# Up projection of a conv-GLU block: seven block products for eight over six of its sixteen contraction tiles, and low weight parts made by adding transfers

## Chip, cores and metric

One core of a Trainium2 chip runs the kernel. The metric is the time of one execution on the device in microseconds (us); the value shown is the median of three runs. Smaller is better.

## The reference

The layer has a token-mixing half and a gated MLP with a convolution. The change touches the MLP, over 512 latent tokens (8 rows of 64), model width 2048 and inner width 5632:

```python
z = h @ w_up                                   # (512, 2048) @ (2048, 11264)
grid = z.reshape(1, rows, GRID_W, 2 * D_FF)
grid = depthwise_3x3(grid, w_conv)             # per channel, SAME padding
val, gate = jnp.split(grid.reshape(1, n, 2 * D_FF), 2, axis=-1)
f_lat = (val * jax.nn.silu(gate)) @ w_down     # (512, 5632) @ (5632, 2048)
```

Ahead of it stand the modulation vectors from the conditioning, the input projection, pooling heads, a diagonal state-space scan and an output projection. After it stand a norm, a gate and the residual. The modulation vector that gates the MLP's output is needed only at the very end; its products run in the background of the MLP.

## The kernel before

**Split numbers.** Each large product is made of two-part operands: `hi` is the value rounded to TensorE's float32r form, `lo` the rest. `mm3` (L175) issues three matmuls for each pair of tiles: hi by hi, hi by lo, lo by hi. An activation tile `h2[k]` (16 of them, one for each contraction tile of 128) holds [hi, lo] of 128 rows by 512 tokens. A matmul has a stationary 128x128 weight tile and, in the MLP, 512 moving columns; only the first two passes of the MLP, whose token halves become ready one after the other (`up_half`), use 256 columns.

**Weight pages.** `Stream` hands weights out in pages of 128x1024 in one fixed order. `load` issues the DMA of a raw page on SP's queue. `make` rounds it on ScalarE into `whi` (L77), and VectorE subtracts to give `wlo` (L78). Rings of two buffers each hold `raw`, `whi` and `wlo`. `get` returns a page and first makes the one behind it (`ahead` 1), so a page is made while its predecessor is multiplied, in the buffers that the page two before it leaves.

**The MLP.** Channels go in 44 passes of 128 value and 128 gate channels. Pass i, `up(i)`, takes four pages (two for the value channels j=0, two for the gate channels j=1), 96 matmuls in all, into one PSUM bank for each j; ScalarE copies each bank into a padded image `zp` (L1345). `conv(i)` runs nine taps for each j on VectorE (L1309, L1311), then silu, product and split into `g`. Every fourth pass completes a group for the down projection: `down(gi, d)` takes two pages and 48 matmuls into four banks, and `evict` adds these to `facc` (L1359). From pass 5 on, one `down` stands behind nearly every `up`.

**Order.** Each engine runs its instructions in program order. TensorE's are written by `up` and `down`; the rest are generators (`Threads`) that get steps at `bg.tick(us)`, `share` (0.65 in the MLP) of the time given, by priority. PSUM has eight banks that rotate. `gemv5` streams the last modulation weights through four `gv` buffers (SP's queue, VectorE dots at L975), and `rows_of` spreads the result to `frow`.

Of the kernel before, what the change touches and what calls it, by code (L numbers as in the profile page):

```python
# [21 lines left out]
F32 = mybir.dt.float32  # L22
# [18 lines left out]
NGRP = NP // GRP  # L41


class Stream:


    def __init__(self, nc, pool, pages, ahead, dahead, bufs):
        self.nc, self.pool, self.pages, self.ahead, self.dahead = nc, pool, pages, ahead, dahead
        self.bufs = bufs
        self.raws, self.made, self.i = [], [], 0  # L50

    def load(self, upto):
        while len(self.raws) < min(upto, len(self.pages)):
            key, ap = self.pages[len(self.raws)]
            n = ap.shape[-1]
# [6 lines left out]

    def make(self, upto):
        nc = self.nc
        while len(self.made) < min(upto, len(self.pages)):
# [3 lines left out]
            n = ap.shape[-1]  # L69
            raw = self.raws[i]  # L70
            self.raws[i] = None
            if key[0] in ("df", "wo2"):
# [57 lines left out]
def emit(tc, A, out, xs_dram, dbg=None):  # L130
# [38 lines left out]

    def gvload(ap):  # L170
        r = ring.tile([128, 512], F32, name="gv", tag="gv", bufs=4)
        nc.sync.dma_start(r[:], ap)
        return r

    def mm3(o, ahi, alo, bhi, blo, start, stop):  # L175
        PE.matmul(o, ahi, bhi, start=start, stop=False)  # L176
        PE.matmul(o, ahi, blo, start=False, stop=False)  # L177
        PE.matmul(o, alo, bhi, start=False, stop=stop)  # L178

# [25 lines left out]
    for x in sched:  # L205
        if x[0] == "U" and x[1] >= NH:
            pages += [(("up", x[1], j), A["w_up"][x[1], j]) for j in range(4)]
# [3 lines left out]
    W = Stream(nc, ring, pages, 1, 1, (2, 2, 2))  # L211
    W.big = lambda name, dt=F32R: sb.tile([128, 1024], dt, name=name, tag="pg", bufs=NPG)
# [4 lines left out]
    pa = phA.enter_context(tc.tile_pool(name="pa", bufs=1))  # L217
    ph0 = ExitStack()
# [748 lines left out]
    def gv_dots(todo, row):  # L967

        tiles = []
        for x in range(len(todo)):  # L970
            while len(tiles) < min(x + 4, len(todo)):
# [105 lines left out]
    def rows_of(c, r, pool, tag, bufs):  # L1077
        dgs = pool.tile([128, 1024], F32, name="dg", tag=tag, bufs=bufs)
        for q in range(4):
            o = bank("rowb")  # L1080
            for k in range(4):
                dg = dgs[:, ((4 * q + k) % 8) * 128:((4 * q + k) % 8 + 1) * 128]
                V.tensor_scalar(dg, ident[:], acol[:, c, 4 * q + k:4 * q + k + 1], None, op0=OP.mult)
            yield 1.0, 0.3
            for k in range(4):
                dg = dgs[:, ((4 * q + k) % 8) * 128:((4 * q + k) % 8 + 1) * 128]
# [195 lines left out]

    frow = [pg(f"frow{j}", (2, 512)) for j in range(2)]

    def gemv5():
        for hf in range(2):
            sr = p2.tile([128, 1024], F32, name="srow2", tag="srow2", bufs=1)
            nc.sync.dma_start(sr[:], A["c_row"][:, hf * 1024:(hf + 1) * 1024])
            S.activation(sr[:], sr[:], AF.Silu)
            todo = [(3, nt, 2 * hf + q) for nt in range(16) for q in range(2)]  # L1290
# [256 lines left out]
```

## Time and profile before

| what | value |
|---|---|
| median of three runs | 2179.85 us (2173.26 to 2180.87) |
| the profiled execution | 2177.72 us |
| its span, first to last instruction | 2175.9 us |
| mean granted TensorE clock | 0.983 |
| busy share: PE, DVE, ACT, POOL | 97%, 69%, 32%, 11% |
| HBM read | 302.46 MB |

PE is TensorE's matmuls and PEld its weight loads, DVE is VectorE, ACT ScalarE, POOL GpSimd, SP the engine that issues most loads. A busy time counts an instruction from its start to its end; matmuls overlap, so the distance between two starts, not the duration of one, says what a matmul costs in a stream. The profiled execution lies 2.1 us under the median of the three runs.

### The profile page before, as it was taken

How to read it: one execution, taken by the hardware profiler on the slowest of the kernel's cores; microseconds unless marked ns; L12 is line 12 of the kernel's file. 1: busy time of each engine (PE TensorE's matmuls, PEld its weight loads, DVE VectorE, ACT ScalarE, POOL GpSimd, SP SyncE). 2: the span in 40 equal slices, each digit the busy share in tenths (PEclk: the TensorE clock that was granted, in tenths of full speed). 3: DMA queues.
4: the chain of work that ended last, by engine and by line, in shares of the span. 5: the costliest groups of instructions: out<-in, count | busy, mean ns of one | idle time of the engine just before them, and what ended most of it. 6: DMA issues, size and time to landing. Idle time of an engine off the chain costs nothing.

```text
span 2175.9 us, 25243 instructions
## 1 busy us (share of the span) xinstructions
PE 2102.5 (97%) x9708; PEld 1645.7 (76%) x9708; DVE 1493.3 (69%) x2183; ACT 694.4 (32%) x976; POOL 243.8 (11%) x311
## 2 busy tenths in 40 slices
PE   7998999999898999999999999999999999999996
PEld 3575777767777888888888888888888888888885
DVE  1573488436677788778778777676776767767676
ACT  3343424544356323322222222222222222222224
POOL 5951100142025000000000000000000000000004
PEclk8999999999999999999999999999999999999998
DMA  9876454657665223443343333232332233232225
GB/s 371 311 285 218 136 178 145 205 150 206 223 211 204 78 88 127 144 140 119 109 154 124 124 126 112 88 97 88 97 97 92 93 97 93 92 97 97 92 93 193
DMA packets 107672, 315.05 MB, mean 145 GB/s; under 512 B 15520, under 2 KB 21536, under 8 KB 103328
## 3 DMA queue, kind: packets, MB, share of 16 engines
q1 hardware_dynamic: 99776, 303.39, 42.0%
q10 hardware_dynamic: 7776, 10.06, 1.4%
q8 instruction: 76, 1.25, 0.2%
q14 instruction: 44, 0.36, 0.0%
HBM read 302.46 MB, written 10.94 MB: 144 GB/s over the span
## 4 chain that ended last, share of the span: by engine, by line
PE 65%; DVE 2%; ACT 1%; issue 1%; DMA 1%; DVEq 0%; POOL 0%; ACTq 0%
PE up L176 14%; PE up L178 14%; PE up L177 14%; PE dn L177 7%; PE dn L178 7%; PE dn L176 7%; ACT scr L1124 1%; DMA raw<-in_w_up 0%; PE uh L178 0%; DMA raw<-in_w_down 0%; DVE facc L1126 0%; PE uh L177 0%; PE uh L176 0%; DVE wlo L78 0%; DVE hf L1195 0%
## 5 line engine op out<-in xcount | busy, mean ns | idle before, releaser
L78 DVE TENSOR_TENSOR wlo<-raw,whi 128x1024 fp32r<-128x1024 f32 (+1 forms) x326 | 403.6, 1239 | 456.7 <-ACT whi L77 453.9
L77 ACT ACTIVATE whi<-raw 128x1024 fp32r<-128x1024 f32 (+1 forms) x326 | 341.5, 1048 | 787.2 <-PE dn L178 308.6
L1311 DVE SCALAR_TENSOR_TENSOR cv<-zp,wconv,cv 128x512 f32<-128x512 f32 x704 | 528.4, 751 | 18.8
L176 PE MATMUL up<-h,whi 128*128 128x512 f32 x1344 | 531.4, 395 | 0.0
L178 PE MATMUL up<-h,wlo 128*128 128x512 f32 x1344 | 530.9, 395 | 0.0
L177 PE MATMUL up<-h,whi 128*128 128x512 f32 x1344 | 530.8, 395 | 0.0
L178 PEld LDWEIGHTS up<-h,wlo 128*128 128x128 f32 x1344 | 251.9, 187 | 61.8
L176 PEld LDWEIGHTS up<-h,whi 128*128 128x128 f32 x1344 | 252.0, 187 | 61.4
L177 PEld LDWEIGHTS up<-h,whi 128*128 128x128 f32 x1344 | 251.9, 187 | 61.4
L177 PE MATMUL dn<-wlo,g 128*128 128x512 f32 x672 | 265.5, 395 | 0.0
L178 PE MATMUL dn<-whi,g 128*128 128x512 f32 x672 | 265.4, 395 | 0.0
L176 PE MATMUL dn<-whi,g 128*128 128x512 f32 x672 | 265.4, 395 | 0.0
L1126 POOL TENSOR_TENSOR facc<-facc,frow 128x512 f32<-128x512 f32 x11 | 15.4, 1422 | 1435.1 <-ACT scr L1124 1435.1
L1345 ACT ACTIVATE zp<-up 128x512 f32<-128x512 f32 x84 | 50.5, 601 | 378.5 <-PE up L178 378.5
L177 PEld LDWEIGHTS dn<-wlo,g 128*128 128x128 f32 x672 | 126.0, 187 | 30.8
L176 PEld LDWEIGHTS dn<-whi,g 128*128 128x128 f32 x672 | 125.9, 187 | 30.9
L178 PEld LDWEIGHTS dn<-whi,g 128*128 128x128 f32 x672 | 126.0, 187 | 30.7
L975 DVE SCALAR_TENSOR_TENSOR scr<-gv,srow 128x512 bf16<-128x512 f32 x132 | 97.4, 738 | 17.8 <-DMA gv<-in_ada_n 11.1
L1359 DVE TENSOR_TENSOR facc<-facc,dn 128x512 f32<-128x512 f32 x144 | 92.1, 680 | 0.7 <-PE dn L178 0.7
L176 PE MATMUL ub<-hT,whi 128*128 128x512 f32 x192 | 79.4, 414 | 1.9 <-ACT mt L585 1.9
L176 PE MATMUL wo<-whi,mx 128*128 128x512 f32 x192 | 79.5, 414 | 0.0
L177 PE MATMUL wo<-wlo,mx 128*128 128x512 f32 x192 | 77.4, 403 | 0.9 <-DVE wlo L78 0.9
(285 smaller groups left out, 2434.4 us busy)
## 6 DMA issues: line engine op xcount, KB each, us to landing
raw<-in_w_up SPq DMA_DIRECT2D x176, 512.0 KB
raw<-in_w_down SPq DMA_DIRECT2D x88, 512.0 KB
gv<-in_ada_n SPq DMA_DIRECT2D x132, 256.0 KB
adak<-in_ada_k SPq DMA_DIRECT2D x32, 1024.0 KB
gv<-in_ada_m SPq DMA_DIRECT2D x96, 256.0 KB
raw<-in_w_out SPq DMA_DIRECT2D x32, 512.0 KB
raw<-in_w_inp SPq DMA_DIRECT2D x24, 512.0 KB
adag<-in_ada_n SPq DMA_DIRECT2D x7, 1024.0 KB
```

Source lines behind the costliest of these rows:

```text
L77: nc.scalar.activation(hi[:, :n], raw[:, :n], AF.Copy)
L78: nc.vector.tensor_tensor(lo[:, :n], raw[:, :n], hi[:, :n].bitcast(F32), op=OP.subtract)
L176: PE.matmul(o, ahi, bhi, start=start, stop=False)
L177: PE.matmul(o, ahi, blo, start=False, stop=False)
L178: PE.matmul(o, alo, bhi, start=False, stop=stop)
L975: V.scalar_tensor_tensor(scr[:, :512], tiles[x][:], 1.0, row(qf), op0=OP.mult, op1=OP.mult, accum_out=gacc[:, qf, c, nt:nt + 1])
L1124: S.activation(scr[:, :512], m, AF.Square, accum_out=st8[:, t, d:d + 1])
L1126: eng.tensor_tensor(m, m, row[d // 2][:, d % 2, :], op=OP.mult)
L1311: V.scalar_tensor_tensor(a[:], zz, wcol, a[:], op0=OP.mult, op1=OP.add)
L1345: S.activation(zp[j][i % 2][:, 1:9, 1:65], o.rearrange("p (r c) -> p r c", r=8), AF.Copy)
L1359: V.tensor_tensor(f, f, os[t], op=OP.add)
```

## The change

**Seven products.** From pass 4 on (`NS`), `up7(i)` replaces `up(i)`. Ten of the 16 contraction tiles are multiplied as before (`plain`, four pages of 640 columns, 15 matmuls each). The other six are taken as three pairs; over value and gate channels, the two tiles of a pair and the two token halves of 256 this is a product of 2x2 blocks, done in Winograd's form with seven block products instead of eight (`half`, seven calls of nine matmuls with 256 columns). The sums of activation blocks are made once on POOL (`hsums`), those of weight blocks for each pass on VectorE, in place in the raw tiles (`make` after `sb`). The seven products go to four banks, and `csums` combines these into `zp`: one ScalarE copy and six VectorE adds in place of two ScalarE copies.

A pass now takes eight pages: up0 (640 columns), sa (768), up2, sb (384 of its 768 made), up1, up3, sA and sB (768 each, the summed blocks). The raw blocks of the pairs come in two tiles of their own (`load_pair`), loaded behind the making of the former pass's sB.

**Low parts.** For up, dn, sa and sb pages VectorE no longer subtracts: ScalarE writes the negated rounded page into `wlo`, and a transfer issued by POOL adds the page from DRAM onto it. For sA and sB (and the pages before the MLP) VectorE still subtracts.

**Order of matmuls.** `page_mm`, and `down` likewise, first issues all hi-by-hi and hi-by-lo matmuls of a page (two thirds), then all that read `wlo`.

**Room.** `gv` goes from four buffers to two, the second `cv` tile from two to one, `rows_of` and `gemv5` work in smaller pieces, and `frow` is made after the last pass.

The core of the diff (the fitting of buffers, layouts of the weights and the moved `frow` are left out):

```diff
 class Stream:
...
-            nc.scalar.activation(hi[:, :n], raw[:, :n], AF.Copy)
-            nc.vector.tensor_tensor(lo[:, :n], raw[:, :n], hi[:, :n].bitcast(F32), op=OP.subtract)
+            nc.scalar.activation(hi[:, c0:n], raw[:, c0:n], AF.Copy)
+            if key[0] in ("up", "dn", "sa", "sb"):
...
+                nc.scalar.activation(lo[:, c0:n], raw[:, c0:n], AF.Copy, scale=-1.0)
+                nc.gpsimd.dma_start(lo[:, c0:n], ap[:, c0:n], accum_op=OP.add)
+            else:
+                nc.vector.tensor_tensor(lo[:, c0:n], raw[:, c0:n], hi[:, c0:n].bitcast(F32), op=OP.subtract)
             self.made.append((key, hi, lo))
+            if key[0] == "sb":
...
+                nc.vector.tensor_tensor(a22, a21, a22, op=OP.add)
+                nc.vector.tensor_tensor(a21, a11, a21, op=OP.subtract)
+                nc.vector.tensor_tensor(a11, a22, a11, op=OP.subtract)
+                nc.vector.tensor_tensor(a12, a12, a11, op=OP.subtract)
+            nxt = self.pairs.get(key)
+            if nxt is not None:
+                self.load_pair(*nxt)
...
+    def page_mm(todo, start, stop):
...
+        for x, (o, ah, al, bh, bl) in enumerate(todo):
+            PE.matmul(o, ah, bh, start=start and x == 0, stop=False)
+            PE.matmul(o, ah, bl, start=False, stop=False)
+        for x, (o, ah, al, bh, bl) in enumerate(todo):
+            PE.matmul(o, al, bh, start=False, stop=stop and x == n - 1)
...
+    def hsums(late):
...
+        for p in range(SW):
+            k1, k2 = h2o[p], h2o[SW + p]
...
+            def full(o, h, c):
+                PO.tensor_tensor(o, h[:, 0, c].bitcast(F32), h[:, 1, c].bitcast(F32), op=OP.add)
+
+            def split(d, x):
+                PO.tensor_copy(d[:, 0], x)
+                PO.tensor_tensor(d[:, 1], x, d[:, 0].bitcast(F32), op=OP.subtract)
+            full(w[0], k1, H0)
+            full(w[1], k1, H1)
+            if late:
+                PO.tensor_tensor(w[0], w[1], w[0], op=OP.subtract)
+                split(k1[:, :, H1], w[0])
+                continue
+            full(w[2], k2, H1)
+            yield 0.0, 0.3
...
+    def csums(i, bk):
...
+        S.activation(z0[:, ha], v(p16[:, H0]), AF.Copy)
+        V.tensor_tensor(z1[:, ha], z0[:, ha], v(p16[:, H1]), op=OP.add)
+        V.tensor_tensor(z0[:, hb], z1[:, ha], v(p57[:, H0]), op=OP.add)
+        yield 0.7, 0
+        V.tensor_tensor(z1[:, ha], z1[:, ha], v(p57[:, H1]), op=OP.add)
+        V.tensor_tensor(z1[:, hb], z1[:, ha], v(p57[:, H0]), op=OP.add)
+        yield 0.7, 0
+        V.tensor_tensor(z0, z0, v(p23), op=OP.add)
+        yield 0.7, 0.3
+        V.tensor_tensor(z1, z1, v(yy), op=OP.add)
...
+    def up7(i):
...
+        plain(p23, 0, 0)
+        w = W.get(("sa", i))
+        half(p16[:, H0], w, 0, lambda p: h2o[p][:, :, H0], True, False)
+        half(p23[:, H0], w, 1, lambda p: h2o[SW + p][:, :, H0], False, False)
+        bg.tick(1.5)
+        plain(yy, 1, 0)
+        w = W.get(("sb", i))
+        half(yy[:, H0], w, 1, lambda p: tt["p", p][2], False, False)
+        bg.tick(0.7)
+        plain(p23, 0, 1)
+        plain(yy, 1, 1)
+        w = W.get(("sA", i))
+        half(p16[:, H1], w, 0, lambda p: tt["p", p][1], False, True)
+        half(p23[:, H1], w, 1, lambda p: h2o[SW + p][:, :, H1], False, True)
+        bg.tick(1.5)
+        w = W.get(("sB", i))
+        half(p57[:, H0], w, 1, lambda p: h2o[p][:, :, H1], True, False)
+        half(p57[:, H1], w, 0, lambda p: tt["p", p][0], False, True)
+        bg.tick(1.0)
+        cth[i] = bg.add(csums(i, bk), 1)
...
     for x in sched:
...
+            if x[1] == NH:
+                hs_t = bg.add(hsums(False), 0)
+            if x[1] == NS - 1:
+                bg.finish(hs_t)
+                W.load_pair(NS, [A["w_ups"][0, m] for m in range(2)])
+            if x[1] == NS:
+                bg.finish(bg.add(hsums(True), 0))
+                g5_t = bg.add(gemv5(), 3)
```

## Rows read from the trace of the kernel before

**Rows 1.** The profile's page: busy time, share of the span, instructions of each engine.

```profile
PE 2102.5 (97%) x9708; PEld 1645.7 (76%) x9708; DVE 1493.3 (69%) x2183; ACT 694.4 (32%) x976; POOL 243.8 (11%) x311
```

**Rows 2.** Busy time by stretch (us, instructions), granted clock, DMA share, GB/s.

```profile
core 0: us, PE busy (x) PEld busy (x) DVE busy (x) ACT busy (x) POOL busy (x), PEclk, DMA share, GB/s
640.00:724.00 84.00, 73.64 (x507) 67.45 (x506) 57.47 (x90) 52.41 (x91) 36.23 (x40) 0.94 0.49 181
724.00:2122.00 1398.00, 1398.00 (x6009) 1123.80 (x6009) 1036.57 (x1423) 365.75 (x445) 0.00 (x0) 1.00 0.33 107
2122.00:2176.00 54.00, 35.69 (x155) 28.70 (x153) 36.26 (x55) 22.56 (x46) 24.44 (x15) 0.86 0.53 195
1500.00:1800.00 300.00, 300.00 (x1287) 241.02 (x1286) 209.13 (x269) 74.62 (x90) 0.00 (x0) 1.00 0.30 95
```

**Rows 3.** PE in order of time: 512-column matmuls, twelve starts apart.

```profile
1830.34 0.40 PE L176 MATMUL dn<-whi,g 128*128 128x512 f32 x1
...
1832.91 0.39 PE L178 MATMUL dn<-whi,g 128*128 128x512 f32 x1
1833.14 0.40 PE L176 MATMUL up<-h,whi 128*128 128x512 f32 x1
```

**Rows 4.** All engines in order of time: 256-column matmuls, nine starts apart.

```profile
702.24 0.28 PE L176 MATMUL uh<-h,whi 128*128 128x256 f32 x1
...
703.29 0.28 PE L176 MATMUL uh<-h,whi 128*128 128x256 f32 x1
```

**Rows 5.** ScalarE, then VectorE, then SP in order of time: making a page, next load.

```profile
1833.34 1.06 ACT L77 ACTIVATE whi<-raw 128x1024 fp32r<-128x1024 f32 x1 [4.54 <-PE dn L178]
1834.43 1.23 DVE L78 TENSOR_TENSOR wlo<-raw,whi 128x1024 fp32r<-128x1024 f32 x1 [0.73 <-ACT whi L77]
1824.97 0.33 SPq L60 DMA_DIRECT2D raw<-in_w_up  x1
```

**Rows 6.** Busy time by stretch around that load, the only one under way.

```profile
1824.90:1825.90 1.00, 1.00 (x6) 0.78 (x5) 0.96 (x3) 0.00 (x0) 0.00 (x0) 1.00 0.00 0
1825.90:1826.40 0.50, 0.50 (x4) 0.40 (x3) 0.50 (x1) 0.00 (x0) 0.00 (x0) 1.00 1.15 180
...
1827.40:1827.90 0.50, 0.50 (x4) 0.41 (x3) 0.50 (x1) 0.16 (x1) 0.00 (x0) 1.00 0.67 270
1827.90:1828.40 0.50, 0.50 (x4) 0.41 (x3) 0.47 (x2) 0.50 (x1) 0.00 (x0) 1.00 0.00 0
```

**Rows 7.** Groups of instructions: ScalarE's copies by form.

```profile
L77 ACT ACTIVATE whi<-raw 128x1024 fp32r<-128x1024 f32 x318 | 336.0, 1057 | 776.1 <-PE dn L178 308.6 <-PE up L177 180.8 <-issue 133.9
L77 ACT ACTIVATE whi<-raw 128x768 fp32r<-128x768 f32 x4 | 3.4, 846 | 9.1 <-PE pp L177 5.3 <-PE ub L177 3.8
L1323 ACT ACTIVATE g<-cv 128x512 fp32r<-128x512 f32 x44 | 27.1, 617 | 5.5 <-DVE cv L1318 5.5
```

**Rows 8.** Groups of instructions: POOL's 256- and 512-column operations.

```profile
L1197 POOL TENSOR_TENSOR h<-hf,h 128x256 fp32r<-128x256 f32 x30 | 25.9, 899 | 15.6 <-ACT h L1193 15.5
L1126 POOL TENSOR_TENSOR facc<-facc,frow 128x512 f32<-128x512 f32 x11 | 15.4, 1422 | 1435.1 <-ACT scr L1124 1435.1
```

**Rows 9.** Groups of instructions of VectorE, 724 to 2122 us.

```profile
L78 DVE TENSOR_TENSOR wlo<-raw,whi 128x1024 fp32r<-128x1024 f32 x249 | 305.1, 1225 | 313.0 <-ACT whi L77 310.3
L1359 DVE TENSOR_TENSOR facc<-facc,dn 128x512 f32<-128x512 f32 x144 | 92.1, 680 | 0.7 <-PE dn L178 0.7
L1309 DVE TENSOR_SCALAR cv<-zp,wconv 128x512 f32<-128x512 f32 x88 | 42.3, 481 | 0.0
```

**Rows 10.** The page's DMA queues: packets, MB, share of 16 engines.

```profile
q1 hardware_dynamic: 99776, 303.39, 42.0%
q10 hardware_dynamic: 7776, 10.06, 1.4%
q8 instruction: 76, 1.25, 0.2%
q14 instruction: 44, 0.36, 0.0%
```

**Rows 11.** The chain that ended last, end of the kernel: start, us, what.

```profile
2127.66 3.45 DMA raw<-in_w_down
2131.13 1.07 ACT wbh L77
```

More of the change, by code (lines that the diff above doesn't have):

```diff
@@ L41 @@
 NGRP = NP // GRP
+SW = 3
+PW = (16 - 2 * SW) * 64
+NS = 4
+ORD = [*range(SW), *range(8, 8 + SW), *range(SW, 8), *range(8 + SW, 16)]
 class Stream:
@@ L970, in gv_dots @@
         for x in range(len(todo)):
-            while len(tiles) < min(x + 4, len(todo)):
+            while len(tiles) < min(x + gvp[1], len(todo)):
                 c, nt, qf = todo[len(tiles)]
@@ L1300, in conv @@
         for j in range(2):
+            while i > 1 - j and not cth[i - 2 + j][2]:
+                bg._step(cth[i - 2 + j])
             z = zp[j][i % 2]
-            a = p2.tile([128, 8, 64], F32, name=f"cv{j}", tag=f"cv{j}", bufs=2)
+            a = p2.tile([128, 8, 64], F32, name=f"cv{j}", tag=f"cv{j}", bufs=2 - j)
             ct = 44 * j + i
@@ L1327, in conv, with v @@
         yield 0.6, 0
-    cth, zfree = {}, set()
+    h2o = [h2[k] for k in ORD]
+    ev_t = []
+    cth, zfree, summed = {}, set(), set()
+    def csums(i, bk):
+        p16, p23, p57, yy = bk
+        bk.clear()
+        z0, z1 = [zp[j][i % 2][:, 1:9, 1:65] for j in range(2)]
+        ha, hb = slice(0, 4), slice(4, 8)
+        def v(a):
+            return a.rearrange("p (r c) -> p r c", c=64)
+        yield 0.0, 0.4
+        for j in range(2):
+            while (i - 2, j) not in zfree:
+                bg._step(cth[i - 2])
+        S.activation(z0[:, ha], v(p16[:, H0]), AF.Copy)
[8 more added lines that the diff above has]
+        V.tensor_tensor(z1, z1, v(yy), op=OP.add)
+        summed.add(i)
+        del p16, p23, p57, yy
+        yield 0.7, 0
+        yield from conv(i)
@@ new lines, in up7, with half, plain @@
+    def up7(i):
+        if i - 1 >= NS:
+            while i - 1 not in summed:
+                bg._step(cth[i - 1])
+        bk = [bank(f"u7{n}") for n in range(4)]
+        p16, p23, p57, yy = bk
+        def half(o, key, m, hs, start, stop):
+            whi, wlo = key
+            cs = [slice((m * SW + p) * 128, (m * SW + p + 1) * 128) for p in range(SW)]
+            page_mm([(o, whi[:, c], wlo[:, c], hs(p)[:, 0], hs(p)[:, 1]) for p, c in enumerate(cs)], start, stop)
+        def plain(o, j, n):
+            whi, wlo = W.get(("up", i, 2 * j + n))
+            nk = PW // 128
+            hs = [h2o[2 * SW + n * nk + k] for k in range(nk)]
+            page_mm([(o, whi[:, k * 128:(k + 1) * 128], wlo[:, k * 128:(k + 1) * 128], h[:, 0, :], h[:, 1, :])
+                     for k, h in enumerate(hs)], n == 0, j == 1 and n == 1)
+            bg.tick(3.3)
+        plain(p23, 0, 0)
[18 more added lines that the diff above has]
+        cth[i] = bg.add(csums(i, bk), 1)
+        if i == NP - 1:
+            h2[:] = [None] * KT
+            h2o.clear()
+            tt.clear()
+            frow.extend(pg(f"frow{j}", (2, 512)) for j in range(2))
+            fr2.append(bg.add(frows(), 0))
@@ L1331, in up, with frows @@
+    fr2 = []
+    def frows():
+        bg.finish(g5_t)
+        while NP - 1 not in summed:
+            bg._step(cth[NP - 1])
+        yield from rows_of(3, frow, p2, "srow2", 1)
     def up(i):
@@ L1367, in down @@
         if gi == NGRP - 1:
-            bg.finish(g5_t)
+            bg.finish(*fr2)
+        bg.finish(*(ev_t if fr2 else ev_t[:-1]))
         os = [bank(f"dn{t}") for t in range(4)]
```

124 lines of the change are left out of this document (93 added, 31 removed).

## The prediction

> **What bounds the kernel now.** I read the busy times on the page of the profile first, then the same split by stage, then instructions in order of time. The page of the profile gives PE 97% of the span, VectorE 69%, ScalarE 32% and POOL 11% [rows 1]. The stretches show where that is exact: from 724 to 2122 us, the MLP, PE is busy for 1398.00 of 1398.00 us at a granted clock of 1.00, while VectorE works 74%, ScalarE 26% and POOL not at all [rows 2]. So in this stage nothing but PE's own stream sets the time, and time won or lost in that stream counts in full. The duration of a matmul record (0.40 us) is not its price: twelve 512-column matmuls start within 2.80 us (1830.34 to 1833.14), 0.2333 us each [rows 3]. The change stands or falls with the price of 256 columns, and the first two passes show it: nine such matmuls, each with its own weight load, start within 1.05 us, 0.1167 us each, exactly half [rows 4].
>
> **The saving.** The six contraction tiles cost a pass 6 x 2 x 3 = 36 matmuls of 512 columns, 8.40 us; they now cost 7 x 9 = 63 of 256, 7.35 us. That is 1.05 us a pass, 42.0 us over the 40 passes from 4 to 43. The ten plain tiles keep their 60 matmuls (14.0 us). Reordering a page's matmuls changes their number nowhere.
>
> **What it asks of VectorE, ScalarE and memory.** For a pass and its `down`, VectorE loses six subtractions of 1.225 us (7.35 us) [rows 9]. It gains two of 768 columns (0.92 each by size), four weight sums of 384 (0.5 each by size), four half-image adds (0.4 each, about half of 0.68) and two whole ones (0.68): 6.8 us. So VectorE stays near 74%. ScalarE gains for low parts four copies of 640 columns, one of 768, one of 384 and two of 1024 (0.73, 0.85, 0.50, 1.06 us, by size between [rows 7]): 6.4 us in about 32.5, from 26% to some 45%. Late in the MLP the DMA engines move 95 GB/s at a share of 0.30 [rows 2]; the adding transfers bring about 3 MB more for each pass and its `down`, so the bandwidth stays. Each of these hides behind PE; what decides is whether a page's parts arrive in time.
>
> **When a low part must be there.** The ring has two `wlo` buffers. The low part of page n can be begun only when page n-2 has had its last matmul, and is needed when page n has done its first two thirds. So the time allowed is the length of page n-1 plus two thirds of page n. The lengths are 3.50 us for a 640-column page, 2.10 for 768 half-width columns, 1.05 for sb, 5.60 for a down page. This gives: sa 3.50 + 1.40 = 4.90; up2 2.10 + 2.33 = 4.43; sb 3.50 + 0.70 = 4.20; **up1 1.05 + 2.33 = 3.38**; up3 5.83; first down page 2.10 + 3.73 = 5.83; second down page 9.33; up0 behind it 7.93. sA and sB still go by VectorE: 1.0 us of copying and subtracting each in place of a transfer. The tight one is up1, behind the short sb.
>
> **What it takes.** ScalarE starts 0.20 us after the stream has gone on from the last matmul (1833.14 to 1833.34), and the next engine 0.03 us after ScalarE's end (1834.40 to 1834.43) [rows 5]. With a copy of 0.73 and the same small handing-over at the end, a 640-column page needs 0.98 us plus D, the time of the adding transfer. No POOL transfer stands in this trace (its queues are two hardware ones and two small instruction ones [rows 10]), so D is bounded by the nearest rows. A plain 512 KB load that SP issues at 1824.97 moves nothing up to 1825.90 and has moved all by 1827.90 [rows 5, 6]: 0.93 us ahead of the packets, 2.0 us of packets. Lower bound for 320 KB: 0.93 + 1.25 = 2.2 us. Upper bound: the old values must be fetched as well as the new, so packets twice as long (2.5), and POOL's work on issuing as long as its largest routine operation, 1.42 us [rows 8]: 4.85 us. I take 2.9 us, the 512 KB row itself: by bytes the adding of 320 KB lies between 320 and 640 KB read, and 512 KB is the row nearest to that.
>
> With D = 2.9 up1 needs 3.88 us where 3.38 are allowed: PE waits 0.50 us a pass, 20 us over 40 passes. The others fit, with the packet time scaled by size: sa 0.20 + 0.85 + 0.05 + 3.3 = 4.4 under 4.90, up2 3.88 under 4.43, sb 2.9 under 4.20, the first down page 0.20 + 1.06 + 0.05 + 4.1 = 5.4 under 5.83. ScalarE, in order, has behind each such copy the next page's copies and a silu or split of 0.62 us; these come late by the same wait, but have a page's length to spare.
>
> The Trainium skill bears on D: "DMA: Bandwidth & Descriptors", section "Anatomy of one DMA — SWDGE (gpsimd) path", fits a transfer issued by GpSimd as 2.0 us plus its bytes over 436 GB/s. For 320 KB that is an estimate of 2.75 us, a wait of 0.35 us a pass, 14 us in all, and 2159 us where I get 2165. The Trainium skill does not say what adding costs on top; no run here shows either.
>
> **Starting the sums.** `hsums` puts 42 POOL operations of 256 columns (0.9 us each [rows 8], 38 us) under passes 2 and 3, which last 45 us. POOL issues the low parts of those passes' pages from the same queue, so one can find up to six operations (5.4 us) ahead of it, against an allowance of 9.3 us: I count 2 us. The 15 later ones (13.5 us) must wait before their first write for pass 3's third page, 5.6 us before its end, and sa of pass 4 is issued behind them: about 6 us after the end, plus 3.3 of transfer and handing over, against 4.90, so 5 us. Together 7 us, between 0 and 15.
>
> **PSUM and the end.** The four banks of a pass are used again a pass later, with `down`'s 11.2 us between. `csums` is a chain of some 3 us on VectorE, so the banks come free in time if VectorE reaches it within 8 us. `frow` is made during the last down blocks (16 small matmuls, as before): nothing. The stretch behind 2122 us keeps its loads, of which one is 3.45 us from release to use [rows 11], against my 2.9.
>
> **Sum.** The profiled execution took 2177.72 us, 1.8 over its span and 2.1 under the median. 2177.72 - 42.0 + 20 + 7 = 2162.7; beside the median of 2179.85, **2165 us**. Half a per cent (11 us) is about what a measurement of this kernel can tell from no change.
>
> **Rivals.**
>
> *Nearly balanced.* With D from 3.0 to 3.3 us (packets 1.7 to 1.9 times as long) up1 waits 0.6 to 0.9 us a pass and, at the upper end, the first down page 0.2: 24 to 43 us with 7 at the start against 42 saved, 2169 to 2190 us. The 3.45 us of [rows 11], though for 512 KB among other loads, speaks for it.
>
> *Low parts come late, and it is slower.* The place is TensorE's wait for `wlo` in the last third of a page; it decides from D = 3.3 us. With packets twice as long and 0.6 us for POOL, D is 4.0: up1 waits 1.60, sa 0.73, both 40 times, the first down page 1.01, 37 times, together 130 us: 2275 us. With the upper bound, 4.85 us: sa 1.55, sb 0.4, up1 2.05, down page 1.8: 228 us, 2373 us. For it: the old values must be fetched, and nothing in this trace shows POOL issuing fast. Against it: the load's own packets left the engines idle a good part of their 2 us (shares 1.15 to 0.67 [rows 6]).
>
> *The banks come late.* If VectorE reaches `csums` only when `down` is over, PE waits for the chain, 2.7 us a pass over 37 passes: 100 us more, 2265 us. Against it: VectorE's load does not grow.
>
> *VectorE holds POOL up.* The first tap is VectorE's fast operation, 481 ns for 512 columns [rows 9], twice a pass. If POOL cannot prepare a transfer while one runs, the tight page comes up to 0.48 us later, 40 times: 19 us more, 2184; with a second tight page hit, 2203. The Trainium skill, "SBUF — State Buffer", section "SBUF: two separate sides", warns of this: VectorE in its two-port mode keeps GpSimd from writing a transfer's descriptors. No POOL transfer here shows it. The taps fill 3% of the time, so few would be hit.
>
> *It does not save.* That half-width matmuls cost more than half is excluded by [rows 4] while PE stays at full clock; PE is granted 0.94 where it often waits (640 to 724 us) [rows 2], but waits of half a microsecond are far shorter than those there.
>
> **How the numbers follow.** Forecast (D up to 3.0 us, faster): 0.44, its own range 2140 (D = 2.2, no waits, nothing lost at the start) to 2169. Nearly balanced: 0.17. Low parts late: 0.31. Banks late: 0.04. VectorE in POOL's way: 0.04, half of it within half a per cent, half above. So faster 0.44, same 0.19, slower 0.37. Eight in ten lie from 2140 to 2265 us: up to D of about 3.9, which leaves out the longer transfers.
>
> **What would show it.** Right: 63 matmuls of 256 columns a pass, 0.1167 us apart; PE waiting a few tenths of a microsecond on the DMA into `wlo` in up1's last third and next to nowhere else; a one-time gap near pass 4. Wrong: waits on that DMA in sa, up1 and the first down page of 1 us and more (D too small), waits for VectorE at a pass's first matmul (banks), a granted clock under 1.00 in the MLP, or ScalarE's low copies themselves held up by silu or by weight sums that VectorE has not yet made.

## The result and the profile after

The change takes 2748.26 us (median of four runs, 2741.63 to 2753.14) where the kernel before takes 2178.41 us on the same chip: ratio 1.2618, 95% interval 1.2581 to 1.2654. 2165 us were predicted, within 2140 to 2265. It is slower by 570 us, three times the loss of the worst case that the prediction worked out (2373 us). At the end of the experiments stands a version that keeps the seven products and takes 2162.13 us, 0.9929 (0.9913 to 0.9945) of before; one of its six executions took 7109 us and is left out of that ratio, and no profile of that execution was kept.

Lines from the page of the profile after, to be held against [rows 1, 10]: busy time of each engine, the transfers' own queue, and the POOL transfers with their size and median time from issue to landing.

```profile
PE 2263.4 (82%) x10788; PEld 1776.5 (65%) x10788; DVE 1492.5 (54%) x2411; ACT 990.4 (36%) x1430; POOL 577.4 (21%) x700
...
q0 software_dynamic: 47808, 124.28, 26.9%
...
wlo<-in_w_up POOLq DMA_DIRECT2D x160, 320.0 KB, 5.4
...
wlo<-in_w_down POOLq DMA_DIRECT2D x84, 512.0 KB, 7.4
```

PE is no longer busy throughout, though it has 42 us less to do. VectorE's busy time is what it was (1492.5 for 1493.3). The transfers land 5.4 and 7.4 us after their issue; the prediction took 2.9 and 4.1.

Busy time by stretch, the columns of [rows 2]; the MLP now reaches from 724 to about 2690 us:

```profile
640.00:724.00 84.00, 73.62 (x504) 66.76 (x502) 58.42 (x92) 53.22 (x92) 37.95 (x43) 0.94 0.51 182
724.00:2690.00 1966.00, 1558.65 (x7088) 1256.37 (x7088) 1032.11 (x1647) 659.02 (x895) 332.48 (x387) 0.90 0.62 139
2690.00:2748.00 58.00, 35.94 (x154) 28.37 (x152) 35.07 (x55) 23.56 (x47) 25.20 (x16) 0.87 0.58 199
1500.00:1800.00 300.00, 244.43 (x1116) 197.57 (x1115) 153.78 (x244) 100.93 (x136) 44.03 (x51) 0.90 0.62 139
```

The whole loss is in the MLP: 1966 - 1398 = 568 us. The work asked for 1398 - 42 = 1356 us of PE at full clock, so 610 us are to be explained. PE stood idle for 1966.00 - 1558.65 = 407 us, and the work took 1558.65 - 1356 = 203 us longer than at full clock (granted 0.90 on average).

Where PE stood idle between 800 and 2600 us (what waited, for what; total us, times, longest):

```profile
PE u L226 <- DMA wlo<-in_w_up: 132.0, 45, 4.5
PE dn L1571 <- DVE facc L1547: 90.9, 32, 4.1
PE u L226 <- DMA wlo<-in_w_ups: 86.0, 58, 10.0
PE dn L1569 <- DMA wlo<-in_w_down: 42.1, 27, 4.8
```

That is 260 us of waiting for low parts, and 91 us of `down` waiting for banks that VectorE had not yet added into `facc`. Outside this stretch PE waits 15.9 us for low parts ahead of 800 us, and behind 2600 us it stands 32.26 us for the row's diagonal tiles (L1145) and 3.9 for a low part. One page shows a wait and what comes with it, PE in order of time:

```profile
1538.05 0.28 PE L223 MATMUL u<-ts,whi 128*128 128x256 f32 x1
...
1538.63 0.28 PE L224 MATMUL u<-ts,whi 128*128 128x256 f32 x1
...
1541.42 0.40 PE L223 MATMUL u<-h,whi 128*128 128x512 f32 x1
1541.65 0.39 PE L224 MATMUL u<-h,whi 128*128 128x512 f32 x1
1544.39 2.07 PE L226 MATMUL u<-h,wlo 128*128 128x512 f32 x5 [2.35 <-DMA wlo<-in_w_up]
1546.25 0.63 PE L223 MATMUL u<-h,whi 128*128 128x512 f32 x1
1546.68 0.63 PE L224 MATMUL u<-h,whi 128*128 128x512 f32 x1
...
1548.37 0.40 PE L224 MATMUL u<-h,whi 128*128 128x512 f32 x1
```

Six 256-column starts lie within 0.58 us, 0.117 each, as in [rows 4]. Then up1 has done its ten hi matmuls and stands 2.35 us for its low part. Behind the wait two 512-column starts lie 0.43 us apart instead of 0.23. The transfer, on POOL:

```profile
1539.28 0.86 POOL L103 DMA_DIRECT2D wlo<-in_w_up  x1 [2.96 <-DMA wlo<-in_w_ups]
```

Issued at 1539.28, awaited until 1544.39: 5.1 us. The granted clock around it (PE busy, clock, DMA share, GB/s) falls to half (1.2 of 2.4 GHz) after the wait and is back some 4 us later:

```profile
1542.00:1544.00 2.00, 0.04 (x1) 1.00 1.05 200
1544.00:1546.00 2.00, 1.61 (x5) 0.73 0.72 134
1546.00:1548.00 2.00, 2.00 (x7) 0.50 0.00 0
1548.00:1550.00 2.00, 2.00 (x9) 0.92 0.66 189
```

The ten matmuls from 1544.39 to 1548.37 take 3.98 us, where ten at 0.2333 are 2.33: this wait costs its 2.35 us and 1.65 more. In this pass PE waits 2.46 us for the banks, 1.49 in the first down page, 1.58 in sa, 0.18 in sb and 2.35 in up1: 8.06 us. A pass with `down` is 32.6 us of matmuls (33.67 before, less 1.05); this one lasts 45.2. The clock fell with the wait of 1.49 us and with the one of 2.35, not with the one of 1.58; of the 119 waits of 1.5 us and more between 800 and 2600 us, 81 were followed by it within 3 us.

The wait for the banks has a longer history. Of the four additions that free `down`'s banks VectorE does one right behind the block, two after the 18 taps of the pass, and the last behind the product that follows the taps (L1425). SP, ScalarE, VectorE and PE in order of time:

```profile
1501.82 5.34 SPq L74 DMA_DIRECT2D rs<-in_w_ups  x2
1507.21 0.42 SPq L68 DMA_DIRECT2D raw<-in_w_down  x1
1511.30 1.06 ACT L97 ACTIVATE whi<-raw 128x1024 fp32r<-128x1024 f32 x1 [1.75 <-DMA raw<-in_w_down]
1513.21 0.61 ACT L1423 ACTIVATE cv<-cv 128x512 f32<-128x512 f32 x1
1513.86 0.69 DVE L1425 TENSOR_TENSOR cv<-cv,cv 128x512 f32<-128x512 f32 x1 [3.62 <-ACT cv L1423]
1514.47 0.68 DVE L1547 TENSOR_TENSOR facc<-facc,dn 128x512 f32<-128x512 f32 x1
1515.20 0.50 PE L1571 MATMUL dn<-whi,g 128*128 128x512 f32 x1 [2.46 <-DVE facc L1547]
```

VectorE is not busy here: it stands idle for 3.62 us, because its product needs ScalarE's silu (L1423). The silu stands behind the two copies of the second down page, and these wait for that page's load. SP issues that load behind the next pass's pair blocks (`load_pair`), of which the second waits until sB is made: from 900 to 2000 us SP waits there 48 times, 312.1 us in all. VectorE is idle for 3.45 to 5.24 us ahead of that product in all 32 bank waits between 800 and 2600 us. In the kernel before no wait of ScalarE for a down page's load is seen from 900 to 2000 us.

### The profile page after: what moved, and what is told of

It reads as the page before. It is cut to its first block, busy times and chain, and to the rows that moved or that the text cites. A ratio compares the mean times of both kernels' runs of the same rounds, so it can differ in the third digit from the quotient of the medians.

```text
span 2747.5 us, 29589 instructions
## 1 busy us (share of the span) xinstructions
PE 2263.4 (82%) x10788; PEld 1776.5 (65%) x10788; DVE 1492.5 (54%) x2411; ACT 990.4 (36%) x1430; POOL 577.4 (21%) x700
## 3 DMA queue, kind: packets, MB, share of 16 engines
q0 software_dynamic: 47808, 124.28, 26.9%
## 5 line engine op out<-in xcount | busy, mean ns | idle before, releaser
L226 PE MATMUL u<-h,wlo 128*128 128x512 f32 (+1 forms) x1280 | 329.9, 382 | 209.4 <-DMA wlo<-in_w_up 132.0
L97 ACT ACTIVATE whi<-raw 128x1024 fp32r<-128x1024 f32 (+2 forms) x326 | 290.7, 892 | 565.1 <-PE u L224 163.9
L223 PE MATMUL u<-h,whi 128*128 128x512 f32 (+1 forms) x1280 | 469.9, 378 | 0.0
L224 PE MATMUL u<-h,whi 128*128 128x512 f32 (+1 forms) x1280 | 465.3, 374 | 0.0
L226 PEld LDWEIGHTS u<-h,wlo 128*128 128x128 f32 x1280 | 226.4, 200 | 277.1 <-DMA wlo<-in_w_up 158.3
L97 ACT ACTIVATE whi<-rs 128x768 fp32r<-128x768 f32 (+1 forms) x160 | 122.6, 767 | 584.3 <-PE u L224 447.9
L223 PEld LDWEIGHTS u<-h,whi 128*128 128x128 f32 x1280 | 264.7, 207 | 42.0
L224 PEld LDWEIGHTS u<-h,whi 128*128 128x128 f32 x1280 | 262.5, 205 | 41.3
L102 ACT ACTIVATE wlo<-raw 128x640 fp32r<-128x640 f32 (+1 forms) x252 | 214.0, 849 | 187.2 <-PE dn L1569 133.6
L103 POOL DMA_DIRECT2D wlo<-in_w_up x168 | 146.5, 872 | 590.5 <-ACT wlo L102 497.7
L105 DVE TENSOR_TENSOR wlo<-rs,whi 128x768 fp32r<-128x768 f32 x80 | 76.7, 959 | 232.1 <-PE u L226 229.7
L105 DVE TENSOR_TENSOR wlo<-raw,whi 128x1024 fp32r<-128x1024 f32 (+1 forms) x74 | 94.7, 1283 | 137.2 <-ACT whi L97 137.0
```

Of the source, the lines that this page charges most:

```text
L97: nc.scalar.activation(hi[:, c0:n], raw[:, c0:n], AF.Copy)
L102: nc.scalar.activation(lo[:, c0:n], raw[:, c0:n], AF.Copy, scale=-1.0)
L103: nc.gpsimd.dma_start(lo[:, c0:n], ap[:, c0:n], accum_op=OP.add)
L105: nc.vector.tensor_tensor(lo[:, c0:n], raw[:, c0:n], hi[:, c0:n].bitcast(F32), op=OP.subtract)
L223: PE.matmul(o, ah, bh, start=start and x == 0, stop=False)
L224: PE.matmul(o, ah, bl, start=False, stop=False)
```

## Experiments

Ratios are to the kernel before on the same chip, with their 95% intervals. The kernel before took 2173 to 2178 us beside all of them.

| run | us | ratio |
|---|---|---|
| change | 2748.26 | 1.2618 (1.2581 to 1.2654) |
| e1 all low parts by VectorE | 2425.54 | 1.1155 (1.1138 to 1.1171) |
| e2 eight products, adding transfers | 2349.70 | 1.0807 (1.0788 to 1.0827) |
| e3 low parts by POOL | 2503.12 | 1.1509 (1.1487 to 1.1531) |
| e4 plain transfers | 2478.57 | one run |
| e5 e1, `facc` first | 2221.94 | 1.0214 (1.0186 to 1.0242) |
| e6 change, `facc` first | 2768.22 | 1.2701 (1.2671 to 1.2730) |
| e7 a mixture | 2400.86 | 1.1035 (1.1005 to 1.1065) |
| e8 e5, row early | 2224.20 | 1.0222 (1.0198 to 1.0245) |
| e9 e8, from pass 7 | 2206.49 | 1.0138 (1.0115 to 1.0162) |
| e10 change, three buffers | 2386.82 | 1.0985 (1.0945 to 1.1025) |
| e11 its two-buffer twin | 2805.20 | 1.2873 (1.2825 to 1.2921) |
| e12 e9, row spread | 2225.47 | 1.0222 (1.0204 to 1.0241) |
| e13 e12, up pages early by transfer | 2199.55 | 1.0127 (1.0111 to 1.0144) |
| e14 e13, row's loads ahead | 2162.13 | 0.9929 (0.9913 to 0.9945) |

**e1: the products without the transfers.**

```diff
-            if key[0] in ("up", "dn", "sa", "sb"):
+            if False:
```

> The changed kernel with all low parts subtracted by VectorE (no negated copy, no adding transfer), seven products kept. Theory A (the adding transfers, 5.4 us to landing for 320 KB, are the whole loss): TensorE's waits for wlo vanish, the granted clock of the MLP goes back to 1.00, and the 42 us of the seven products show unless VectorE, which gets 7 us more work for each pass and its down block (about 32 of 32.5 us), becomes the bound: 2140 to 2230 us. Theory B (the shape of the new passes, with sums and PSUM banks waiting for VectorE, costs as much as the transfers): 2350 us or more, with waits of the first down matmul for VectorE of 90 us and more kept.

323 us of the loss go and 251 stay, as theory B had it. PE now waits in the passes for one thing alone (900 to 2100 us):

```profile
PE dn L1571 <- DVE facc L1547: 128.8, 29, 6.0
```

VectorE's order is part of it: after the sums of a pass it does all 18 taps, and only then two of the four `facc` additions that free `down`'s banks. `evict` and the thread of sums and taps have the same priority, and the thread was there first; in the kernel before the taps ran at a lower one. The late load is the other part: ahead of those additions VectorE subtracts a low part for the second down page, and its wait for ScalarE's `whi` of that page takes 73.4 of the 128.8 us. In one such wait, from 1630 to 1632 us, neither PE nor VectorE works; the same wait and the clock behind it, in the columns of [rows 2]:

```profile
1630.00:1632.00 2.00, 0.00 (x0) 0.00 (x0) 0.06 (x1) 1.15 (x2) 0.00 (x0) 1.00 0.86 299
1632.00:1634.00 2.00, 0.18 (x1) 0.18 (x2) 2.00 (x3) 0.43 (x1) 0.00 (x0) 0.69 0.02 6
1634.00:1636.00 2.00, 2.00 (x5) 1.63 (x6) 2.00 (x4) 0.00 (x0) 0.00 (x0) 0.50 0.54 164
...
1638.00:1640.00 2.00, 2.00 (x7) 1.58 (x6) 0.00 (x0) 0.60 (x1) 0.00 (x0) 0.60 0.03 8
1640.00:1642.00 2.00, 2.00 (x10) 1.60 (x9) 0.54 (x1) 0.93 (x3) 0.00 (x0) 1.00 0.00 0
```

**e2: the transfers without the products.** The kernel before with the negated copy and the adding transfer for its `up` and `dn` pages, and the change's order of matmuls.

```diff
-            nc.vector.tensor_tensor(lo[:, :n], raw[:, :n], hi[:, :n].bitcast(F32), op=OP.subtract)
+            if key[0] in ("up", "dn"):
+                nc.scalar.activation(lo[:, :n], raw[:, :n], AF.Copy, scale=-1.0)
+                nc.gpsimd.dma_start(lo[:, :n], ap[:, :n], accum_op=OP.add)
```

> The kernel before with eight products and full pages of 5.6 us, but with the negated copy on ScalarE and the adding transfer for the low parts of all up and down pages, and with the low matmuls last in each page. Theory A with the allowance rule (page n-1 plus two thirds of page n, 9.3 us here, against 0.2 + 1.1 + 7.4 = 8.7 us needed): little or no waiting, 2180 to 2230 us. Theory A': the transfers cost whatever the pages are (by engines or queues that they load): 2350 us or more. Theory B: same as before, 2170 to 2190 us.

Slower by 175 us, with VectorE 48% busy (577.55 of 1200 us): at the lower edge of theory A'. Its issues on the page and PE's waits from 900 to 2100 us:

```profile
wlo<-in_w_up POOLq DMA_DIRECT2D x168, 512.0 KB, 7.7
```

```profile
PE up L191 <- DMA wlo<-in_w_up: 46.6, 49, 2.4
PE dn L1390 <- DMA wlo<-in_w_down: 36.4, 30, 2.6
```

With pages of 5.60 us each the allowance is 9.33 us. In a wait followed along its chain ScalarE's copies to `zp` (0.60), `whi` (1.05) and `wlo` (1.05) stand in line ahead of a transfer of 7.99: 10.7 us. So the transfers are late without the short pages of the change too, here together with ScalarE's line ahead of them.

**e3 and e4: what in a transfer costs.** e3 lets POOL subtract; e4 leaves the adding out of the transfer, so that `wlo` then holds weights and the output is another one.

```diff
e3
-                nc.scalar.activation(lo[:, c0:n], raw[:, c0:n], AF.Copy, scale=-1.0)
-                nc.gpsimd.dma_start(lo[:, c0:n], ap[:, c0:n], accum_op=OP.add)
+                nc.gpsimd.tensor_tensor(lo[:, c0:n], raw[:, c0:n], hi[:, c0:n].bitcast(F32), op=OP.subtract)
e4
-                nc.gpsimd.dma_start(lo[:, c0:n], ap[:, c0:n], accum_op=OP.add)
+                nc.gpsimd.dma_start(lo[:, c0:n], ap[:, c0:n])
```

> The changed kernel with the low parts of up, dn, sa and sb pages subtracted by POOL (tensor_tensor of raw and hi, about 2.4 us for 1024 columns and 1.5 for 640 by the rows of before) in place of copy and transfer. Theory A: a low part is there 1.7 us after its buffer is free, under every allowance, so the saving shows: 2135 to 2165 us, if POOL and VectorE do not hold each other up; if they do (VectorE's taps have two inputs in SBUF), VectorE's chain becomes the bound: 2180 to 2300 us. Theory B: 2350 us or more.

> The changed kernel with POOL's transfer made plain, without the adding (so wlo holds the rounded weights and the output is another): the price of adding against that of a transfer from POOL as such. If adding is what is slow (packets twice as long or more), a 320 KB transfer lands in about 3 us in place of 5.4 and the time falls by 150 us or more, to 2300 to 2600 us; if the way through POOL is slow, it stays at 5 us and 2650 us or more.

e4's page:

```profile
q0 software_dynamic: 47808, 124.28, 15.9%
...
wlo<-in_w_up POOLq DMA_DIRECT2D x160, 320.0 KB, 3.6
...
wlo<-in_w_down POOLq DMA_DIRECT2D x84, 512.0 KB, 4.6
```

The same packets and bytes take 15.9% of 2476.8 us where adding takes 26.9% of 2747.5: 739 for 394 us, 1.88 times as long. Adding costs 1.8 us for 320 KB and 2.8 for 512 KB; a plain one from POOL is at 3.6 us already 1.4 above the bound of 2.2 that was drawn from SP's load. That load was the only one under way, and these are not: how much of the 1.4 us is POOL's way and how much the loads beside it, no run separates. e4 lies in the range expected if adding is what is slow; but even plain, it is 304 us above before: from 900 to 2000 us PE waits 73.6 us for low parts and 67.5 for banks. The Trainium skill, "DMA: Bandwidth & Descriptors", section "Anatomy of one DMA — SWDGE (gpsimd) path", gives 2.0 us and bytes over 436 GB/s, an estimate of 2.75 us; the trace does not agree, with 3.6 us plain and 5.4 adding.

e3 lies above both ranges of theory A. In it POOL's low parts are in time, and the loss is VectorE's: 112.3 us of waits for banks from 900 to 2000, in which VectorE is idle for under 2. Its group of taps from 900 to 2000 us, in e3 and then in the change:

```profile
L1417 DVE SCALAR_TENSOR_TENSOR cv<-zp,wconv,cv 128x512 f32<-128x512 f32 x440 | 529.3, 1203 | 12.7
```

```profile
L1418 DVE SCALAR_TENSOR_TENSOR cv<-zp,wconv,cv 128x512 f32<-128x512 f32 x379 | 284.6, 751 | 10.9
```

A tap takes 1203 ns on average while POOL subtracts and 751 ns while it only issues transfers. The Trainium skill, "SBUF — State Buffer", section "Who interferes with whom", says that a VectorE instruction with two inputs in SBUF contends with a GpSimd instruction that reads SBUF; e3 agrees. VectorE's taps are not slowed by the change's transfers: they took 751 ns before too.

**e5 and e6: the down sums first**, in e1 and in the change.

```diff
-        ev_t.append(bg.add(evict(gi, d, os), 1))
+        ev_t.append(bg.add(evict(gi, d, os), 0))
```

> e1_seven_vector (seven products, all low parts by VectorE) with one number changed: the eviction of a down block gets steps ahead of the new sums and taps (priority 0 in place of 1). Theory B1 (in VectorE's order the facc adds stand behind the taps of a whole pass, so the next down block's banks come late, and each such wait of 4 us is followed by some 5 us at the half clock): the waits of the first down matmul for VectorE, 28 of 4.6 us in 1200 us, vanish, the granted clock of the MLP returns to 1.00, and the time falls from 2425 to 2150 to 2250 us, VectorE with 31.6 us of work in a pass and down block of 32.5 being the next bound. Theory B2 (VectorE is already the bound, whatever the order): the wait moves to another place and the time stays at 2380 us or more.

> The changed kernel, transfers and all, with the same number changed. If the bank waits and the transfers' waits add up, this takes away about 91 us of waiting in 2747 and the half clock behind them (60 to 90 us): 2560 to 2620 us. If the transfers' waits grow by what the bank waits leave (the low part then is late for the same moment), it stays above 2680 us.

Without transfers one digit is worth 204 us, as theory B1 had it: the bank waits are gone. What is left of PE's waits from 900 to 2000 us, and VectorE's own longest wait there:

```profile
PE u L226 <- DVE wlo L105: 10.1, 16, 1.0
```

```profile
DVE wlo L105 <- ACT whi L97: 98.4, 36, 4.0
```

A pass with `down` takes 33.1 us in e5, 0.6 less than before. The 45 us that e5 loses against the kernel before stand elsewhere: at the start of the seven products (from 800 to 900 us PE is busy 86.16 of 100 us) and at the end (PE stands 34.9 us). VectorE's 98.4 us are the late load again: ScalarE waits 138.9 us for loads of down pages (32 times).

With transfers it earns nothing (2768 us, the second of its two cases). There the bank waits go too, and the waits for `in_w_down` are longer instead: 88.5 us from 900 to 2000 against 29.0. That fits a TensorE which, held up in one place, reaches the next transfer later, so e1's and e6's numbers do not add. e6 against e5, the same order, prices the transfers at 546 us.

**e7: transfers for some pages.** e5 with the transfer for the second down page and for up0 only, and the weight sums on POOL.

```diff
-            if False:
+            if (key[0] == "dn" and key[3] == 1) or (key[0] == "up" and key[1] > 5 and key[2] == 0):
...
-                nc.vector.tensor_tensor(a22, a21, a22, op=OP.add)
+                nc.gpsimd.tensor_tensor(a22, a21, a22, op=OP.add)
```

> e5 with less work for VectorE: the adding transfer only where the allowance is long (second down page, 9.3 us, and the first up page, behind it, 7.9 us, against 8.9 and 6.6 needed), and the four sums of weight blocks on POOL. VectorE has some 27 us in 32.5. If VectorE's load is what is left in e5: 10 to 60 us under e5, at best 2145 us. If POOL's reads and VectorE's taps hold each other up, or the transfers delay ScalarE's queue, no better than e5.

Worse than e5 by 179 us. PE waits 97.4 us (29 times, longest 5.2) for the second down page. By the rule it has 9.33 us, but the rule takes the raw page as there, and ScalarE waits 119.2 us (26 times, longest 6.2) for the load of a down page. In the pass around 1515 us that load is issued at 1511.43, right behind the pair blocks; the copy starts at 1515.53 after 4.37 us of waiting, POOL has then been idle for 13.91 us, and PE gets the low part at 1525.84. POOL's sums do not hold the transfer up there, and from 900 to 2000 us POOL waits for ScalarE's copy 55 times (409.2 us) ahead of a transfer. e7 changed two things at once and does not price them apart.

**e8, e9, e12: the row at the end, the sums at the start.** In e5 the row's 64 products (`gemv5`) have the last priority; 46 find time, later on one in each pass, and the last 18 run behind the passes: PE stands 34.9 us. e8 serves them first, 3.5 pages apart; e9 besides begins the seven products at pass 7; e12 serves them 2.5 pages apart and makes the 16 diagonal tiles together.

```diff
e8
-                yield 0.8, 0.5
+                yield 0.8, 3.5
-                g5_t = bg.add(gemv5(), 3)
+                g5_t = bg.add(gemv5(), 0)
e9
-NS = 4
+NS = 7
e12
-                yield 0.8, 3.5
+                yield 0.8, 2.5
-        yield from rows_of(3, frow, p2, "srow2", 1)
+        dgs = [pg(f"fdg{n}") for n in range(2)]
+        ...
```

> The low parts by VectorE and the down sums freed first, as in the run that took 2222 us, and besides: the ada row's products (gemv5) are served at once at a spacing of 3.5 us of matmul time instead of last, so that its row is ready before the last pass ends. Theory (the seven products save their 42 us, and what is left over is two holes, one at the start of the sums and one at the end, where TensorE waits 35 us for the row's diagonal tiles and then runs at half clock): the end wait falls away, 35 to 45 us less, so 2175 to 2190. Rival (VectorE at 89% is the bound, and the row's products only move the wait): 2210 to 2230, with the wait turning up in the passes as waits for banks or low parts.

> The same with the seven products only from pass 7 on, 37 passes in place of 40: it gives up 3 x 1.05 = 3 us of matmuls and leaves the passes without down products, where taps, sums and low parts crowd on VectorE, to the old eight products. Theory (the 10.5 us gap at the start of the sums comes from VectorE overloaded there, and costs 20 to 30 us with the half clock behind it): 2150 to 2170, faster than the kernel before (about 2177). Rival (the gap is the price of making the sums, wherever it is): it moves with the sums, 2178 to 2195.

> Seven products from pass 7, low parts by VectorE, down sums freed first. In the two runs before it the row's 64 products were served 3.5 pages (18 us) apart and so still ended after the last pass: 22.7 us of waiting for the diagonal tiles. Here they come 2.5 pages (13 us) apart, 64 x 13 = 832 us, done near 1760 us, and the 16 diagonal tiles are made together in two pages that the activations have left, 2.5 pages before TensorE multiplies them. Theory (what is left over against the kernel before is that wait and the half clock behind it): 22.7 us and some 10 us of half clock go, 2206 - 30 = 2165 to 2185, the same as the kernel before within 0.5%. Rival (VectorE at 89% is the bound, so the wait comes back as waits for low parts and banks): 2195 to 2210.

(The spacing is counted in pages of 5.2 us; e8's expectation took it for us, and so its row was still late, by 16.2 us.) e8 lies in the range of its rival, e12 above its own rival's, and e9 above both of its ranges. e9 cures the start: PE is busy 98.83 of 100 us from 800 to 900 where e5 has 86.16. e12 cures the end, and its waits there are gone; but a pass with `down` goes from 33.1 us in e5 to 33.6 in e8 and e9 and 35.1 in e12, and from 700 us on PE waits for VectorE in e12 63 times for low parts (39.5 us) and 23 times for banks (12.9). VectorE, 73% busy before (800.43 of 1100 us), is at 89% in e5 (900 to 1200 and on), so that more work in the passes finds little room. But it is not shown that its load is the limit: in e12 VectorE stands idle for 133.8 of the 1100 us until ScalarE has copied a page, and ScalarE waits there 164.5 us for the loads of down pages. A kernel with that load ahead of the pair blocks was not run.

**e10 and e11: a third `wlo` buffer.** The negated copy and the transfer start one page earlier; both have `facc` and the row first, and one buffer in place of two for the row's weights and for `cv0`. e11 is the same with the third buffer unused.

```diff
+        if self.ahead == 1:
+            self.make_lo(self.i + 2)
```

> The changed kernel with its adding transfers, down sums freed first and the row early, and a third buffer of low parts: each negated copy and its transfer start one page earlier than before. To make room the row's weight tiles and the first taps' tile have one buffer in place of two. Theory (the transfers cost because they land 5.4 and 7.4 us after the issue, later than a page ahead allows, and the waits pull the clock to half): with about 4 to 6 us more in hand the waits for low parts go, clock above 0.97, and the time is that of the version with the low parts by VectorE or less, 2170 to 2230. Rival (the transfers cost by what they take from others: the queue serves only so many, or ScalarE's second copy delays its own queue): the waits stay, 2500 or more.

> The same with the third buffer left out, so that the low parts start where the change starts them: the comparison for the run with three. Both theories: near the run of the change with the down sums freed first (2768 us), less up to 40 us for the row at the end, 2700 to 2770.

418 us lie between the two, by the earlier start alone (of the negated copy, the transfer and with them the raw page's load); the transfers' own times are alike (5.4 and 7.8 us for e11's 5.8 and 7.4). e11 itself came out 35 us above its range. PE's waits from 900 to 2000 us, e10 and then e11:

```profile
PE dn L1606 <- DMA wlo<-in_w_down: 62.9, 36, 2.9
PE u L263 <- DMA wlo<-in_w_ups: 11.4, 12, 1.9
PE u L263 <- DMA wlo<-in_w_up: 4.5, 6, 1.4
```

```profile
PE u L263 <- DMA wlo<-in_w_up: 100.7, 32, 4.4
PE dn L1606 <- DMA wlo<-in_w_down: 81.4, 23, 4.3
PE u L263 <- DMA wlo<-in_w_ups: 46.7, 31, 3.2
```

The up pages are cured, the 512 KB of the down pages are not; there ScalarE's negated copy waits 109.9 us (29 times) for the raw page's load. The theory had 2170 to 2230 and got 2387: right in kind, not in size.

**e13 and e14: what the others point to.** e13 is e12 with e10's third buffer: only the four up pages go by early transfer, the rest by VectorE, which loses 4 x 0.82 us a pass. e14 then loads the row's weight tile ahead.

```diff
e13
-        if key[0] not in ("up", "dn", "sa", "sb"):
+        if key[0] != "up":
e14
+            if gvp[1] == 1:
+                yield -1
...
-                yield 0.8, 2.5
+                yield (0.0, 1.5) if x < 0 else (0.8, 1.0)
```

> The version before it (seven products from pass 7, row spread), but the low parts of the four 640-column pages of a pass are made by the adding transfer, started one page earlier in a third buffer; the pages of the down projection and the corner blocks stay with VectorE. It takes 4 x 0.82 = 3.3 us of a 33 us pass from VectorE, some 10% of its time. Theory (two things stood in the way of the 1.05 us that a pass saves: VectorE near 90%, and transfers that land later than their page is wanted; with the load eased and the transfers early neither is left): TensorE above 98% in the passes, 2145 to 2180, the first version level with the kernel before or faster. Rival 1 (transfers cost by themselves, early or not, as the three-buffer run at 2387 may say): 2280 or more. Rival 2 (the loss in the passes is ScalarE's order, which now carries one more copy a page): waits for whi copies, 2200 to 2260.

> The version before it with one thing moved: in it VectorE, eased by the early transfers, stood 130 us in the 1,100 us of the passes (31 times, longest 5.7) waiting for the row's weight tile, which has one buffer and is loaded right before its product. Here the load is issued 1.5 pages (8 us) before the product. Theory (the seven products give back their 1.05 us a pass once VectorE and the low parts are both in time; those 130 us were what the low parts of the down pages and the banks waited for): VectorE's waits for the tile go, TensorE 98% or more in the passes, 2150 to 2180. Rival (ScalarE's one queue, with its extra copy, sets the pace): VectorE's waits go and the time stays, 2190 to 2205.

e13 missed, and its VectorE's waits from 900 to 2000 us say why: the row's tile, with one buffer, is fetched right before its product, and VectorE stands about as long as the transfers had given it (3.3 us in each of 33 passes).

```profile
DVE scr L1070 <- DMA gv<-in_ada_n: 130.5, 31, 5.7
```

e14 moves that load alone, gains 37 us and lies in its theory's range. PE's waits from 700 us to the end, and its stretch from 900 to 2000 us:

```profile
PE u L264 <- DMA wlo<-in_w_up: 8.5, 8, 2.2
PE u L261 <- ACT whi L131: 5.1, 6, 1.1
PE up L261 <- ACT whi L131: 4.1, 2, 2.3
```

```profile
900.00:2000.00 1100.00, 1090.03 (x5704) 920.95 (x5703) 923.20 (x1452) 407.75 (x571) 114.33 (x133) 1.00 0.61 151
```

A pass with `down` takes 33.06 us (34 of them in the 1124 us from 876 to 2000) where it took 33.67. Of the 1.05 us that a pass saves, 0.6 arrive, as in e5. What e14 has over e5 is the start and the end, mended without the passes growing longer; ScalarE still waits 113.4 us there for the loads of down pages.

## Why the prediction was wrong

**The saving of 42.0 us** is right: 256 columns cost 0.117 us in the change too.

**What it takes, D = 2.9 us, failed**, and not within its bounds: 5.4 us, where 4.85 was the upper one. Packets 1.88 times as long were in that bound (2.5 us for 1.25), and POOL's issue (0.86 us) is under the 1.42 allowed. What was missing is the rest of a POOL transfer beside other loads: a plain one lands after 3.6 us, and SP's load had let 2.2 be expected. The row of one queue, alone under way, gave no bound for another. 7.4 us for 512 KB, where 4.1 were taken, followed from the same step. That VectorE holds POOL up is not seen: POOL's issues took 0.86 us, 1.12 at most.

**When a low part must be there** is right as far as the buffers go. With the upper bound the rival "Low parts come late" had sa at 1.55, up1 at 2.05, the first down page at 1.8 and sb at 0.4 us; the pass above shows 1.58, 2.35, 1.49 and 0.18. So close a match is partly luck: the transfers were longer than that bound, and the bank wait of 2.46 us gave the down page's that much more time. That rival had the cause, with a chance of 0.31; its 2373 us counted waits only. What the rule leaves out is the raw page: it is taken as there, and the second down page's was late.

**"Waits of half a microsecond are far shorter than those there" failed with it.** Those for transfers were up to 4.8 us (once 10.0), and after most of the longer ones the granted clock went to 0.50. That is 203 of the 610 us, and no rival had a price for it. The 0.94 of the stretch up to 724 us [rows 2] was read as a reason against; it was the warning.

**The banks** failed. "In time if VectorE reaches it within 8 us" was said of the pass's own four banks, and for these PE does not wait. The banks that came late are `down`'s, which the prediction did not count, and its answer to the rival ("VectorE's load does not grow") was a load where the order decides. VectorE worked no more than before and still came late: the additions that free the banks stood behind the taps and behind a product for which VectorE stood idle until ScalarE, held by a late load, had done its silu. That is 91 us of waits in the change, and 204 us by one digit in e5.

**The end, "`frow`: nothing"**, failed: 32.26 us. Not the 16 small matmuls but the products that lead to them were late: at the last priority they soon got only one turn a pass, and the last 18 ran behind the passes, from 2603 to 2642 us, where all 64 were done by 1345 us before.

**The start, 7 us**, was too small: waits for low parts between 640 and 860 us come to 35.7.

**VectorE near 74%** is right for its work, 1032.11 us in the MLP for 1036.57. Whether the transfers are needed at all stays open. Without them VectorE is at 89%, and e5's passes still keep 0.6 of the 1.05 us; e8, e9 and e12, which mend the start or the end without transfers, lose that again in the passes.

What stays open: what the late load of the second down page costs in each of these versions, since none issues it ahead of the pair blocks; and what e10 has above before, some 210 us, beyond the waits named and the end. A third buffer beside two for the row's weights was not tried.

## What to carry to other kernels

A transfer that stands in for an engine's work takes that work's load but brings its own delay: hold the delay against the buffers' lead, page by page, and give it a page more of lead before counting on the load. In a stream that is busy 100% of the time waits can be paid one and a half times (610 us for 407 here), as the clock falls behind the longer ones; so a saving of 1 us in 33 is soon spent: the one version that came out below the kernel before has 18 us of waits left from 700 us to the end. Ask of each shared engine not only how full it is but what it does first, above all which of its operations frees banks. Where an engine stands idle ahead of such an operation, follow its wait back: here it led over ScalarE to a load that stood in SP's order behind two others.

## What the hardware showed unexpectedly

- With a wait of 2.35 us (change) and of 4.21 us (e1) the granted clock fell to 0.50 and was back at 1.00 some 4 to 6 us after the wait's end; 512-column starts lay 0.43 us apart meanwhile. In e2, with 79 waits of 1.05 us on average and none above 2.6, its mean was 0.99 (900 to 2100 us).
- An adding transfer from POOL: 5.4 us for 320 KB and 7.4 for 512 KB; a plain one 3.6 and 4.6, medians beside other loads. POOL itself is busy 0.86 us with each.
- VectorE's taps: 751 ns beside POOL's transfers, 1203 ns on average beside POOL's subtractions.
